# A filter unit's end given out between the next unit's first pieces, its norm summed in two parts, and one more place for weight preparation

## The chip, the core and the metric

The kernel runs on one core of a Trainium2 chip. The engines that matter here are TensorE (PE, with its weight loads shown apart as PEld), VectorE (DVE), ScalarE (ACT), GpSimd (POOL) and SyncE (SP), which issues most DMA transfers. Each engine works through its own instructions in order and waits on semaphores for the others. The metric is the device time of one execution in microseconds, the median of several runs; lower is better.

## What is computed

The program is a backbone of two layers over 2048 tokens of width 1024 with 256 context tokens. The even layer mixes a pooling branch with attention of 6 query heads over 2 key heads; the odd layer has a long convolution by FFT (Hyena) and a Fourier branch. The change touches the part that makes the filters of the long convolution, and the preparation of the odd layer's weights. Both run in the gaps of the even layer's attention. The filters are:

```python
h = (hdn @ w3).reshape(L, HY_ORDER, 2, HY_WIDTH)        # L 2048, order 2, width 768
h = h * decay[:, None, None, :]
h = h / (jnp.sum(jnp.abs(h), axis=(0, 2), keepdims=True) + EPS)
k = jnp.concatenate([h[:, :, 0], zero, h[:0:-1, :, 1]], axis=0)
...
zf = jnp.fft.rfft(z, n=2 * L, axis=1)
kf = jnp.fft.rfft(k, n=2 * L, axis=0)
return jnp.fft.irfft(zf * kf[None], n=2 * L, axis=1)[:, :L]
```

The norm of a channel, the sum of absolute values over all positions, is needed only at the end of a filter, where it also scales the skip term; the spectrum kf is what is stored for the odd layer.

## The kernel before, in words

The attention runs in 96 blocks (6 heads x 8 groups of rows x 2 halves). Each block is a string of tokens, written by hand in BLOCK: one string for even and one for odd blocks, and two shorter ones for the time when the side work is over. A token is a piece of a block: T transposes probabilities (PE), copies them out as ph (ACT) and takes the rest as pl (DVE); S multiplies scores (PE); M takes the row's highest value (DVE); E takes exponentials (ACT); Z sums them; V multiplies by values; D and N finish a block of rows: D makes the diagonal bdg (ACT) and prb (PE), N makes rb (DVE) and gives y<-rb to SP. At the end of a block SP gets the query loads qh, ql and bsg for a later block. Transposes have six PSUM buffers.

Between these pieces stand three tokens for side work. F (and f, in one pair of blocks out of eight) runs the filter generator up to its next yield, which is called a fill here; p runs one step of the weight preparation. Each engine gets its instructions in the order in which the tokens are reached, so the strings set the order of everything. after(n, fn) leaves a piece of work until n tokens later, or until the next fill at the latest.

The filter generator makes 12 units (6 groups of 128 channels x 2 orders). A unit has 8 groups of positions. For each, PE makes hacc (L1194), DVE multiplies by the decay into ht (L1195, two buffers) and reduces absolute values into one of eight slots of rd (L1198); in a second fill PE makes the first DFT stage fa from ht (L1231) and ACT copies it into fX three tokens later (L1232). At the last group, DVE sums the eight slots into rs (L1204), PE spreads that sum (smacc, L1207 and L1208), DVE makes the scale sc_n and puts the skip term into ht (L1213 to L1218), makes sum and difference sd (L1219, L1220), PE makes fa from sd (L1229), and the last copy fills fX. A unit takes 18 fills. The matmul results hacc, smacc, fa and fnp of all side work share one PSUM buffer.

When fX is complete the rest of its FFT is put on a list of 48 POOL operations, which some() gives out at each fill for an estimated FFT_US of 4.4 us, and FFT_LATE, 4 calls of some() later, SP gets the store spec<-fX (2 MB, L1143). fX has two buffers (FILTER_X), the FFT's intermediate fT one. The skip row skr (512 B) is fetched with the filter weights, two units deep.

The weight preparation multiplies a piece by its gate on POOL, rounds it to wodd on ACT (L1409), takes the rest on POOL and stores wodd (wo, wi); its last part makes fnp on PE from the DFT matrix and the Fourier branch's weights (L1446) and copies it to fnM. When the filter generator is done, fill() runs whatever is left of the preparation at once and then opens the pools for the output projection, whose pieces fill the last blocks.

Of the kernel before, what the change touches and what calls it, by code (L numbers as in the profile page):

```python
# [20 lines left out]
P = 128  # L21
D = 1024
# [4 lines left out]
EPS = 1e-6  # L27
# [9 lines left out]
NCH = HW_ // P  # L37
N2 = 16
# [3 lines left out]
PAIRS = [(n, N2 - n) for n in range(1, 8)] + [(0, 8)]  # L42

BLOCK = [
# [204 lines left out]
def tile_net(ctx, tc, i, k, out, keep=None):  # L249
    nc = tc.nc  # L250
    v, s, g, pe, sy = nc.vector, nc.scalar, nc.gpsimd, nc.tensor, nc.sync
# [36 lines left out]
    specd = [[dram(f"spec{j}_{o}", (P, 2, N2, P)) for o in range(2)] for j in range(NCH)]  # L288
# [211 lines left out]
    with ExitStack() as st, tc.manual_schedule(engines=EVERY):  # L500
        sp = pool(st, "a_sb", 2)
# [617 lines left out]
    def filters(st, psum, tag, after):  # L1119

        fc = pool(st, "f_c2", 1, side="right")
        sp = pool(st, "f_u", 1, side="right")
        dft = fc.tile([P, N2, 2, P], F32, name="fdft")
        late, ops = [], []
        got, room = {}, [0.0]

        def some():

            due[0] += 1
            room[0] = min(room[0] + FFT_US, FFT_US)
            while ops and room[0] > 0:
                us, op = ops.pop(0)
                room[0] -= us
                if callable(op):
                    op()
                else:  # L1140
                    late.append((due[0] + FFT_LATE, op))
            if late and late[0][0] <= due[0]:
                sy.dma_start(*late.pop(0)[1])  # L1143

        due = [0]

        def fetch(u, grp):
            dec = sp.tile([P, 2, P], F32, tag="dec", name="dec", bufs=2)
            sy.dma_start(dec, k["decay"][u // 2, grp])
            hd = sp.tile([P, 2, P], F32R, tag="hd", name="hd", bufs=2)  # L1150
            n, m = PAIRS[grp]
            mv(hd, hdd[:, n : m + 1 : m - n, :])
            got[u, grp] = dec, hd

        def fetch_w3(u):
# [6 lines left out]
            skr = sp.tile([1, P], F32, tag="skr", name="skr", bufs=2)  # L1162
            sy.dma_start(skr, i["hy_skip"][0, o : o + 1, jl])
            got[u] = raw, skr

        def split_w3(u):
            raw, skr = got[u]
# [3 lines left out]
            got[u] = w, skr  # L1171
# [7 lines left out]
        for u in range(2 * NCH):  # L1179
            j, o = u // 2, u % 2  # L1180
            w3, skr = got.pop(u)
            rd = sp.tile([P, 8, P], F32, tag="rd", name="rd")
            X = sp.tile([P, 2, N2, P], F32, tag="X", name="fX", bufs=FILTER_X)
            for grp, (n, m) in enumerate(PAIRS):
                last = grp == 7
                if (u, grp) != (2 * NCH - 1, 7):
                    fetch(u + grp // 7, (grp + 1) % 8)
                dec, hd = got.pop((u, grp))
                ht = sp.tile([P, 2, 2, P], F32, tag="ht", name="ht", bufs=2)
                acc = psum.tile([P, 2, 2, P], F32, tag=tag, name="hacc")  # L1190
                for q in range(2):
                    for x in range(2):
                        w = w3[:, x, ::-1] if q else w3[:, x]
                        pe.matmul(acc[:, q], hd[:, q, :], w, start=x == 0, stop=x == 1)  # L1194
                after(1, lambda: v.tensor_mul(ht, acc, dec.unsqueeze(2).to_broadcast([P, 2, 2, P])))  # L1195
                yield
                some()
                v.tensor_reduce(out=rd[:, grp, :], in_=ht.rearrange("p a d b -> p b (a d)"), axis=AX.X, op=ALU.add,  # L1198
                                apply_absolute_value=True)
                if u + 1 < 2 * NCH and grp in (3, 6):  # L1200
                    (fetch_w3 if grp == 3 else split_w3)(u + 1)
                if last:
                    rs = sp.tile([P, P], F32, tag="rs", name="rs")
                    v.tensor_reduce(out=rs, in_=rd.rearrange("p a b -> p b a"), axis=AX.X, op=ALU.add)  # L1204
                    yield
                    sm = psum.tile([P, 512], F32, tag=tag, name="smacc")
                    pe.matmul(sm[:, 0:1], rs, ones[:, 0:1], start=True, stop=True)  # L1207
                    pe.matmul(sm[0:1, P : 2 * P], ones[:, 0:1], rs, start=True, stop=True)  # L1208
                    sd = sp.tile([P, 2, 2, P], F32, tag="ht", name="sd", bufs=2)

                    def scaled():
                        idx = o * NCH + j
                        v.tensor_scalar(out=sc_n[:, idx : idx + 1], in0=sm[:, 0:1], scalar1=EPS, scalar2=None, op0=ALU.add)  # L1213
                        rw = sp.tile([1, P], F32, tag="rw", name="rw")
                        v.scalar_tensor_tensor(out=rw, in0=sm[0:1, P : 2 * P], scalar=EPS, in1=skr, op0=ALU.add, op1=ALU.mult)
                        v.reciprocal(sc_n[:, idx : idx + 1], sc_n[:, idx : idx + 1])
                        v.tensor_add(ht[0:1, 0, 0, :], ht[0:1, 0, 0, :], rw)
                        v.memset(ht[0:1, 0, 1, :], 0.0)  # L1218
                        v.tensor_add(sd[:, 0], ht[:, :, 0], ht[:, :, 1])  # L1219
                        v.tensor_sub(sd[:, 1], ht[:, :, 0], ht[:, :, 1])  # L1220


                    after(2, scaled)
                    yield
                fa = psum.tile([P, 2, 2, P], F32, tag=tag, name="fa")
                for r in range(2):
                    for q, b in enumerate((n, m)):
                        if last:
                            pe.matmul(fa[:, r, q], dft[:, b, r, :], sd[:, r, q], start=True, stop=True)  # L1229
                        else:  # L1230
                            pe.matmul(fa[:, r], dft[:, b, r, :], ht[:, q], start=q == 0, stop=q == 1)  # L1231
                after(3, lambda: s.copy(X[:, :, n : m + 1 : m - n, :], fa))  # L1232
                yield
                if last:
                    T = sp.tile([P, 2, N2, P], F32, tag="T", name="fT")
                    ops += [(0.04 + 2.05 * us, fn) for fn, us in fft16(g, X, T, False, g, True)]
                    ops.append((0.0, (specd[j][o], X)))
                some()
        while ops or late:
            some()  # L1240
            yield
# [17 lines left out]
    with ExitStack() as st:  # L1259
# [195 lines left out]
        def after(n, fn):  # L1455

            pending.append([n, fn])
# [145 lines left out]
    with ExitStack() as st, tc.manual_schedule(engines=EVERY):  # L1603
# [222 lines left out]
    with ExitStack() as st, tc.manual_schedule(engines=EVERY):  # L1826
# [265 lines left out]
        with ExitStack() as fs:  # L2092
# [75 lines left out]
            for lb in range(2):  # L2168
# [251 lines left out]
```

## Time and profile before

| | before |
|---|---|
| median of 3 runs (lowest, highest) | 3173.49 us (3167.7, 3178.07) |
| profiled execution: time, span | 3180.38 us, 3178.6 us |
| PE busy | 2935.4 us (92%), 16969 instructions |
| PEld busy | 2519.8 us (79%) |
| DVE busy | 2146.7 us (68%) |
| ACT busy | 1325.2 us (42%) |
| POOL busy | 1131.8 us (36%) |
| mean granted clock of TensorE | 0.968 |

The profiled execution is one run with the profiler on; its own time is the 3180.38 us, 6.9 us above the median of the runs without a profile. PE has the largest share, but a share over the whole span says little of one stage. The attention with the filters between its pieces lies between about 620 and 1620 us of the span, the end of the filters, the output projection and the rest of the even layer behind it. What is to be read is the idle time of PE in that stretch, and what released it: in a row of the timeline the brackets name that idle time, the engine that ended it, and the tile and line that it wrote.

### The profile page before, as it was taken

How to read it: one execution, taken by the hardware profiler on the slowest of the kernel's cores; microseconds unless marked ns; L12 is line 12 of the kernel's file. 1: busy time of each engine (PE TensorE's matmuls, PEld its weight loads, DVE VectorE, ACT ScalarE, POOL GpSimd, SP SyncE). 2: the span in 40 equal slices, each digit the busy share in tenths (PEclk: the TensorE clock that was granted, in tenths of full speed). 3: DMA queues.
4: the chain of work that ended last, by engine and by line, in shares of the span. 5: the costliest groups of instructions: out<-in, count | busy, mean ns of one | idle time of the engine just before them, and what ended most of it. 6: DMA issues, size and time to landing. Idle time of an engine off the chain costs nothing. (4 is left out here: it accounts for less than half of the span.)

```text
span 3178.6 us, 46875 instructions
## 1 busy us (share of the span) xinstructions
PE 2935.4 (92%) x16969; PEld 2519.8 (79%) x16969; DVE 2146.7 (68%) x3981; ACT 1325.2 (42%) x3047; POOL 1131.8 (36%) x1091
## 2 busy tenths in 40 slices
PE   7899999799999999999986999999989999988799
PEld 4898888688888888888875778777878787874577
DVE  4676436477777777777764343377789797978556
ACT  4444545365555555555554232322323222232223
POOL 3122222127768787777772344001010000101110
PEclk9999999899999999999998999999999999999899
DMA  6466335533433334333325676688898989876875
GB/s 219 149 203 206 119 134 165 177 98 123 128 124 120 110 121 131 112 107 113 114 77 193 213 265 244 241 267 275 267 310 272 292 280 307 274 251 184 217 206 175
DMA packets 346707, 602.74 MB, mean 190 GB/s; under 512 B 41894, under 2 KB 216168, under 8 KB 336490
## 3 DMA queue, kind: packets, MB, share of 16 engines
q1 hardware_dynamic: 321322, 516.63, 47.8%
q0 software_dynamic: 25152, 83.10, 11.2%
q8 instruction: 134, 2.20, 0.3%
q14 instruction: 99, 0.81, 0.1%
HBM read 376.80 MB, written 187.18 MB: 177 GB/s over the span
## 5 line engine op out<-in xcount | busy, mean ns | idle before, releaser
L312 DVE TENSOR_TENSOR pl<-pt,ph 128x512 fp32r<-128x512 f32 (+1 forms) x480 | 300.1, 634 | 160.0 <-ACT ph L309 153.6
L155 DVE TENSOR_TENSOR gB<-gB 128x256 f32<-128x256 f32 (+3 forms) x442 | 351.6, 845 | 51.5 <-ACT gB L1927 47.7
L1334 ACT ACTIVATE pb<-S,mx 128x512 f32<-128x512 f32 (+1 forms) x480 | 310.7, 658 | 177.5 <-DVE mx L1326 143.3
L315 PE MATMUL dacc<-dh,dw 128*128 128x512 f32 x768 | 311.4, 405 | 46.5 <-DMA dh<-h1T 45.4
L309 ACT CAST ph<-pt 128x512 fp32r<-128x512 f32 (+1 forms) x480 | 256.2, 557 | 216.9 <-PE pt L1345 215.0
L316 PE MATMUL dacc<-dh,dw 128*128 128x512 f32 x768 | 304.4, 396 | 0.0
L317 PE MATMUL dacc<-dh,dw 128*128 128x512 f32 x768 | 304.1, 396 | 0.0
L1323 DVE TENSOR_REDUCE mx<-S 128x1 f32<-128x512 f32 (+1 forms) x480 | 279.5, 629 | 8.9 <-PE S L317 8.7
L1345 PE MATMUL pt<-ident,pb 128*128 128x128 f32 x1728 | 251.3, 275 | 21.4 <-ACT pb L1334 20.0
L312 POOL TENSOR_TENSOR wl<-raw,wh 128x256 fp32r<-128x256 f32 x160 | 134.8, 873 | 373.3 <-ACT wh L309 347.6
L1357 PE MATMUL o<-ph,vh 128*128 128x256 f32 x864 | 237.9, 306 | 0.2
L1345 PEld LDWEIGHTS pt<-ident,pb 128*128 128x128 f32 x1728 | 200.2, 141 | 41.3 <-ACT pb L1334 29.8
L315 PE MATMUL S<-kh,qh 128*128 128x512 f32 (+1 forms) x480 | 200.0, 417 | 30.1 <-DVE pl L312 15.4
L1358 PE MATMUL o<-ph,vl 128*128 128x256 f32 x864 | 220.4, 286 | 1.8 <-DMA vl<-vl 1.8
L155 POOL TENSOR_TENSOR fX<-fT 128x256 f32<-128x256 f32 (+2 forms) x168 | 219.2, 1328 | 2.6
L315 PEld LDWEIGHTS dacc<-dh,dw 128*128 128x128 f32 x768 | 147.7, 192 | 85.0 <-DMA dh<-h1T 43.4
L155 POOL TENSOR_TENSOR fT<-fX 128x1024 f32<-128x1024 f32 (+2 forms) x120 | 190.8, 1622 | 58.4 <-ACT fX L1232 56.6
L315 PE MATMUL acc<-wh,hh 128*128 128x256 f32 x672 | 198.8, 296 | 5.4 <-DVE hh L311 2.6
L317 PE MATMUL acc<-wh,hl 128*128 128x256 f32 x672 | 194.0, 289 | 1.0 <-DVE hl L312 0.9
L316 PE MATMUL acc<-wl,hh 128*128 128x256 f32 x672 | 194.1, 289 | 0.9 <-POOL wl L312 0.8
L316 PE MATMUL S<-kl,qh 128*128 128x512 f32 (+1 forms) x480 | 182.2, 379 | 1.3 <-DMA kl<-kT1l 1.3
L317 PE MATMUL S<-kh,ql 128*128 128x512 f32 (+1 forms) x480 | 181.9, 379 | 0.0
(475 smaller groups left out, 7397.5 us busy)
## 6 DMA issues: line engine op xcount, KB each, us to landing
dh<-h1T SPq DMA_DIRECT2D x172, 512.0 KB
spec<-fX SPq DMA_DIRECT2D x12, 2048.0 KB
dw<-wi SPq DMA_DIRECT2D x48, 512.0 KB
gK<-spec SPq DMA_DIRECT2D x48, 512.0 KB
raw<-in_ev_w_in_dram SPq DMA_DIRECT2D x160, 128.0 KB
u<-dev SPq DMA_DIRECT2D x70, 256.0 KB
cu<-u POOLq DMA_DIRECT2D x17, 1024.0 KB, 8.3
wmb<-in_w_mod_dram SPq DMA_DIRECT2D x16, 1024.0 KB
```

Of the source, the lines that this page charges most:

```text
L155: put(out, lambda: v.tensor_tensor(out=out, in0=in0, in1=in1, op=op))
L309: s.copy(hi, src)
L312: lo_eng.tensor_sub(lo, src, hi.bitcast(F32))
L315: pe.matmul(acc, ah, bh, start=first, stop=False)
L316: pe.matmul(acc, ah, bl, start=False, stop=False)
L317: pe.matmul(acc, al, bh, start=False, stop=last)
L1323: v.tensor_reduce(out=B["mx"][:, c : c + 1], in_=S[:, :n], axis=AX.X, op=ALU.max)
L1334: s.activation(B["pb"][:, c * 512 : c * 512 + n], B["S"][c][:, :n], AF.Exp, bias=B["mx"][:, 5:6], accum_out=B["sm"][:, c : c + 1])
L1345: pe.transpose(pt[:, t, :], B["pb"][:, (4 * c + t) * P : (4 * c + t + 1) * P], ident)
L1357: pe.matmul(gr["o"], vh[:, a, :], ph[:, t, :], start=a == 0, stop=False)
L1358: pe.matmul(gr["o"], vl[:, a, :], ph[:, t, :], start=False, stop=False)
```

## The change

The last group's tail is cut out of its unit. norm (smacc, scale, skip term, sd), the last group's spectrum and the start of the FFT of unit u are now given out between the first pieces of unit u + 1: behind its features(0), behind its spectrum(0), and before its features(1). Only the last unit has its tail by itself. The sum over slots is taken in two parts: at group 4 over slots 0 to 4 into slot 5, at group 7 over the four slots 2 to 5 (later groups reuse slots from 2 on) into slot 0; rd has six slots, and rs is gone. ht has three buffers. The skip row is fetched at group 6, into one buffer. A unit takes 17 fills in place of 18. Even blocks get one more p at their end, so a pair of blocks has seven in place of six.

```diff
 BLOCK = [
-    "T0 p S0 S1 F S2 S3 S4 M T1 f p F D V3 V4 E1 N E3 T2 E0 T3 p E4 E2 F T4 Z",
+    "T0 p S0 S1 F S2 S3 S4 M T1 f p F D V3 V4 E1 N E3 T2 E0 T3 p E4 E2 F T4 p Z",
...
-            rd = sp.tile([P, 8, P], F32, tag="rd", name="rd")
-            X = sp.tile([P, 2, N2, P], F32, tag="X", name="fX", bufs=FILTER_X)
...
-                ht = sp.tile([P, 2, 2, P], F32, tag="ht", name="ht", bufs=2)
...
-                if last:
-                    rs = sp.tile([P, P], F32, tag="rs", name="rs")
-                    v.tensor_reduce(out=rs, in_=rd.rearrange("p a b -> p b a"), axis=AX.X, op=ALU.add)
-                    yield
-                    sm = psum.tile([P, 512], F32, tag=tag, name="smacc")
...
-                    after(2, scaled)
-                    yield
-                fa = psum.tile([P, 2, 2, P], F32, tag=tag, name="fa")
...
+            ht = st_[grp] = sp.tile([P, 2, 2, P], F32, tag="ht", name="ht", bufs=3)
...
+        def sums(st_, grp):
+
+            u, rd = st_["u"], st_["rd"]
+            v.tensor_reduce(out=rd[:, grp - 3 * (grp > 4), :], in_=st_[grp].rearrange("p a d b -> p b (a d)"), axis=AX.X, op=ALU.add,
+                            apply_absolute_value=True)
...
+            if grp == 6:
+                st_["skr"] = fetch_skip(u)
+            if grp in (4, 7):
+                lo, hi, to = (0, 5, 5) if grp == 4 else (2, 6, 0)
+                v.tensor_reduce(out=rd[:, to, :], in_=rd[:, lo:hi].rearrange("p a b -> p b a"), axis=AX.X, op=ALU.add)
...
+            after(2, scaled)
+            after(3, both)
...
+            after(3, lambda: s.copy(X[:, :, n : m + 1 : m - n, :], fa))
...
+        last = None
+        for u in range(2 * NCH + 1):
+            st_ = None
+            if u < 2 * NCH:
+                w3 = got.pop(u)
+                st_ = {"u": u, "w3": w3, "rd": sp.tile([P, 6, P], F32, tag="rd", name="rd")}
+                features(st_, 0)
+            yield
+            some()
+            if last:
+                norm(last)
+                yield
+            if st_:
+                sums(st_, 0)
+                spectrum(st_, 0)
+            if last or st_:
+                yield
+                some()
+            if last:
+                spectrum(last, 7)
...
+                transform(last)
...
+            for grp in range(1, 8):
+                features(st_, grp)
+                yield
+                some()
+                sums(st_, grp)
+                if grp < 7:
+                    spectrum(st_, grp)
+                    yield
+                    some()
+            last = st_
```

On DVE at the end of a unit in the middle of the filters, before (rd and rs are the unit's last sums, L1213 and L1215 its scale; pl, mx, sm and r belong to the attention):

```order
L1198 TENSOR_REDUCE rd<-ht 128x128
L1204 TENSOR_REDUCE rs<-rd 128x128
L312 TENSOR_TENSOR pl<-pt,ph 128x2x128
L1329 TENSOR_REDUCE sm<-sm 128x1
L1330 RECIPROCAL r<-sm 128x1
L312 TENSOR_TENSOR pl<-pt,ph 128x4x128
L1323 TENSOR_REDUCE mx<-S 128x1 x2
L312 TENSOR_TENSOR pl<-pt,ph 128x4x128
L1323 TENSOR_REDUCE mx<-S 128x1 x3
L1326 TENSOR_REDUCE mx<-mx 128x1
L1213 TENSOR_SCALAR sc_n<-smacc 128x1
L1215 SCALAR_TENSOR_TENSOR rw<-smacc,skr 1x128
```

And at such an end now:

```order
L1200 TENSOR_REDUCE rd<-ht 128x128
L1208 TENSOR_REDUCE rd<-rd 128x128
L1195 TENSOR_TENSOR ht<-hacc,dec 128x512
L312 TENSOR_TENSOR pl<-pt,ph 128x4x128
L312 TENSOR_TENSOR pl<-pt,ph 128x2x128
L1380 TENSOR_REDUCE sm<-sm 128x1
L1381 RECIPROCAL r<-sm 128x1
L312 TENSOR_TENSOR pl<-pt,ph 128x4x128
L1374 TENSOR_REDUCE mx<-S 128x1 x3
L1220 TENSOR_SCALAR sc_n<-smacc 128x1
L1222 SCALAR_TENSOR_TENSOR rw<-smacc,skr 1x128
L1223 RECIPROCAL sc_n<-sc_n 128x1
```

The next unit's first ht stands between the sum and the scale now; sd follows in both.

On ACT at the end of the weight preparation, before (wodd is a prepared weight, fnM the Fourier branch's, the rest is attention):

```order
L1334 ACTIVATE pb,sm<-S,mx 128x512
L1334 ACTIVATE pb,sm<-S,mx 128x256
L309 CAST ph<-pt 128x4x128 x2
L1409 CAST wodd<-wraw 128x512 x2
L1448 COPY fnM<-fnp 128x512 x2
L1366 ACTIVATE bdg<-ident,r 128x128 x2
L1334 ACTIVATE pb,sm<-S,mx 128x512 x2
```

Now the last of them stands by itself, one in each of two blocks:

```order
L1385 ACTIVATE pb,sm<-S,mx 128x512
L1385 ACTIVATE pb,sm<-S,mx 128x256
L309 CAST ph<-pt 128x4x128
L1499 COPY fnM<-fnp 128x512
L309 CAST ph<-pt 128x4x128
L1417 ACTIVATE bdg<-ident,r 128x128 x2
L1385 ACTIVATE pb,sm<-S,mx 128x512 x2
```

Four pieces of the preparation that stood in a row at one place of one block are spread over the blocks ahead.

On ACT, the first copy of unit 4 into fX now, with what each waits for (DMAHW is a DMA queue, where the store of unit 2 from the same buffer is meant):

```order
L309 CAST ph<-pt 128x4x128 [waits PE_49,Activation_49]
L1417 ACTIVATE bdg<-ident,r 128x128 x2
L1246 COPY fX<-fa 128x2x2x128 [waits DMAHW6_49,PE_49,Pool_49]
L1385 ACTIVATE pb,sm<-S,mx 128x512 [waits DVE_49]
L1385 ACTIVATE pb,sm<-S,mx 128x512
```

On SP, the rows up to that store:

```order
L261 DMA wi_6_183<-wodd 128x1024 [waits DMAHW7_49,Pool_49]
L1477 DMA wgb<-gate_227 128x512 [waits DMAHW0_49]
L1480 DMA wraw<-in_ev_w_out_dram 128x512 [waits DMAHW1_49]
L261 DMA y_85<-rb 128x256 [waits DMAHW2_49,DVE_49]
L261 DMA qh<-qT1h 128x256 [waits DMAHW3_49,PE_49]
L261 DMA ql<-qT1l 128x256 [waits DMAHW4_49,PE_49]
L1351 DMA bsg<-sg_3_78 128x256 [waits DMAHW5_49]
L1143 DMA spec_0_151<-fX 128x4096 [waits DMAHW6_49]
```

Before, the same store stood thus, and the first copy of the unit that reuses its buffer came in a later block:

```order
L261 DMA qh<-qT1h 128x256 [waits DMAHW1_49,PE_49]
L261 DMA ql<-qT1l 128x256 [waits DMAHW2_49,PE_49]
L1300 DMA bsg<-sg_3_78 128x256 [waits DMAHW3_49]
L261 DMA wi_4_181<-wodd 128x1024 [waits DMAHW4_49,Pool_49]
L497 DMA wraw<-in_od_w_in_dram 128x2x128 [waits DMAHW5_49]
L497 DMA wraw<-in_od_w_in_dram 128x2x128 [waits DMAHW6_49]
L1143 DMA spec_0_151<-fX 128x4096 [waits DMAHW7_49]
```

The copy of the new unit is reached, in the order of tokens, between the last blocks' work and the store's place behind y, qh, ql and bsg; before, it came after the store.

More of the change, by code (lines that the diff above doesn't have):

```diff
@@ L1170, in split_w3, with fetch_skip @@
             v.tensor_sub(w[:, 1], raw, w[:, 0].bitcast(F32))
-            got[u] = w, skr
+            got[u] = w
+        def fetch_skip(u):
+            skr = sp.tile([1, P], F32, tag="skr", name="skr")
+            sy.dma_start(skr, i["hy_skip"][0, u % 2 : u % 2 + 1, u // 2 * P : u // 2 * P + P])
+            return skr
         fetch(0, 0)
@@ L1178, in filters, with features @@
         yield
-        for u in range(2 * NCH):
-            j, o = u // 2, u % 2
-            w3, skr = got.pop(u)
-            rd = sp.tile([P, 8, P], F32, tag="rd", name="rd")
-            X = sp.tile([P, 2, N2, P], F32, tag="X", name="fX", bufs=FILTER_X)
[L1184 to L1188, printed above, removed]
-                ht = sp.tile([P, 2, 2, P], F32, tag="ht", name="ht", bufs=2)
[L1190 to L1195, printed above, removed]
+        def features(st_, grp):
+            u = st_["u"]
+            if (u, grp) != (2 * NCH - 1, 7):
+                fetch(u + grp // 7, (grp + 1) % 8)
+            dec, hd = got.pop((u, grp))
+            w3 = st_["w3"]
+            ht = st_[grp] = sp.tile([P, 2, 2, P], F32, tag="ht", name="ht", bufs=3)
+            acc = psum.tile([P, 2, 2, P], F32, tag=tag, name="hacc")
+            for q in range(2):
+                for x in range(2):
+                    w = w3[:, x, ::-1] if q else w3[:, x]
+                    pe.matmul(acc[:, q], hd[:, q, :], w, start=x == 0, stop=x == 1)
+            after(1, lambda: v.tensor_mul(ht, acc, dec.unsqueeze(2).to_broadcast([P, 2, 2, P])))
@@ new lines, in sums @@
+        def sums(st_, grp):
+            u, rd = st_["u"], st_["rd"]
+            v.tensor_reduce(out=rd[:, grp - 3 * (grp > 4), :], in_=st_[grp].rearrange("p a d b -> p b (a d)"), axis=AX.X, op=ALU.add,
+                            apply_absolute_value=True)
+            if u + 1 < 2 * NCH and grp in (3, 6):
+                (fetch_w3 if grp == 3 else split_w3)(u + 1)
+            if grp == 6:
[3 more added lines that the diff above has]
+                v.tensor_reduce(out=rd[:, to, :], in_=rd[:, lo:hi].rearrange("p a b -> p b a"), axis=AX.X, op=ALU.add)
@@ new lines, in norm, with scaled, both @@
+        def norm(st_):
+            u, ht, rs = st_["u"], st_[7], st_["rd"][:, 0, :]
+            idx = u % 2 * NCH + u // 2
+            sm = psum.tile([P, 512], F32, tag=tag, name="smacc")
+            pe.matmul(sm[:, 0:1], rs, ones[:, 0:1], start=True, stop=True)
+            pe.matmul(sm[0:1, P : 2 * P], ones[:, 0:1], rs, start=True, stop=True)
+            sd = st_["sd"] = sp.tile([P, 2, 2, P], F32, tag="ht", name="sd", bufs=3)
+            def scaled():
+                v.tensor_scalar(out=sc_n[:, idx : idx + 1], in0=sm[:, 0:1], scalar1=EPS, scalar2=None, op0=ALU.add)
+                rw = sp.tile([1, P], F32, tag="rw", name="rw")
+                v.scalar_tensor_tensor(out=rw, in0=sm[0:1, P : 2 * P], scalar=EPS, in1=st_["skr"], op0=ALU.add, op1=ALU.mult)
+                v.reciprocal(sc_n[:, idx : idx + 1], sc_n[:, idx : idx + 1])
+                v.tensor_add(ht[0:1, 0, 0, :], ht[0:1, 0, 0, :], rw)
+                v.memset(ht[0:1, 0, 1, :], 0.0)
+            def both():
+                v.tensor_add(sd[:, 0], ht[:, :, 0], ht[:, :, 1])
+                v.tensor_sub(sd[:, 1], ht[:, :, 0], ht[:, :, 1])
+            after(2, scaled)
+            after(3, both)
@@ new lines, in spectrum @@
+        def spectrum(st_, grp):
+            if "X" not in st_:
+                st_["X"] = sp.tile([P, 2, N2, P], F32, tag="X", name="fX", bufs=FILTER_X)
+            X, (n, m) = st_["X"], PAIRS[grp]
+            fa = psum.tile([P, 2, 2, P], F32, tag=tag, name="fa")
+            for r in range(2):
+                for q, b in enumerate((n, m)):
+                    if grp == 7:
+                        pe.matmul(fa[:, r, q], dft[:, b, r, :], st_["sd"][:, r, q], start=True, stop=True)
+                    else:
+                        pe.matmul(fa[:, r], dft[:, b, r, :], st_[grp][:, q], start=q == 0, stop=q == 1)
+            after(3, lambda: s.copy(X[:, :, n : m + 1 : m - n, :], fa))
@@ new lines, in transform @@
+        def transform(st_):
+            u, X = st_["u"], st_["X"]
+            T = sp.tile([P, 2, N2, P], F32, tag="T", name="fT")
+            ops.extend([(0.04 + 2.05 * us, fn) for fn, us in fft16(g, X, T, False, g, True)])
+            ops.append((0.0, (specd[u // 2][u % 2], X)))
+        last = None
[14 more added lines that the diff above has]
+            if last or st_:
@@ L1196, in filters @@
                 yield
                 some()
[L1198 to L1201, printed above, removed]
-                if last:
-                    rs = sp.tile([P, P], F32, tag="rs", name="rs")
-                    v.tensor_reduce(out=rs, in_=rd.rearrange("p a b -> p b a"), axis=AX.X, op=ALU.add)
-                    yield
-                    sm = psum.tile([P, 512], F32, tag=tag, name="smacc")
[L1207 to L1220, printed above, removed]
-                    after(2, scaled)
-                    yield
@@ L1225, in filters @@
-                fa = psum.tile([P, 2, 2, P], F32, tag=tag, name="fa")
[L1226 to L1232, printed above, removed]
@@ L1233, in filters @@
-                yield
[L1234 to L1238, printed above, removed]
+            if last:
[3 more added lines that the diff above has]
+                some()
+            if st_ is None:
+                break
+            for grp in range(1, 8):
[5 more added lines that the diff above has]
+                    spectrum(st_, grp)
+                    yield
+                    some()
```

6 lines of the change are left out of this document (2 added, 4 removed).

## The prediction

> **What bounds the kernel now.** I read the page's slices first, then the attention stage, which the change touches, in windows.
>
> ```profile
> span 3178.6 us, 46875 instructions
> PE   7899999799999999999986999999989999988799
> 950.00:1000.00 50.00, 49.77 (x335) 45.65 (x334) 37.86 (x75) 29.48 (x78) 49.16 (x40) 1.00 0.30 93
> 1000.00:1050.00 50.00, 47.16 (x316) 41.61 (x315) 39.44 (x77) 27.69 (x73) 34.99 (x23) 1.00 0.41 137
> 1650.00:1700.00 50.00, 34.80 (x213) 29.95 (x211) 24.89 (x53) 21.32 (x57) 35.81 (x34) 0.89 0.36 124
> 1700.00:1750.00 50.00, 35.90 (x215) 31.05 (x216) 20.73 (x44) 21.18 (x55) 1.37 (x2) 0.81 0.59 220
> ```
>
> A windows row gives the stretch, its length, then busy time of PE, weight loads, DVE, ACT and POOL, the granted clock, and the DMA share and GB/s. PE bounds this stage: it is busy 49.8 of 50 us where no filter unit ends, 47.2 where one does, and loses about 15 us in each of the two stretches behind the last unit. So only PE's idle time can be won, and a new wait that reaches PE is paid in full.
>
> **Gain 1: the weight preparation is no longer rushed.** Before, steps of it are left when the filters end, and all are issued at once between two pieces of one block. With seven places in two blocks instead of six it ends beforehand; the last groups then stand among other work (the rows on ACT above).
>
> ```profile
> 1641.37 0.50 PE L315 MATMUL S<-kh,qh 128*128 128x512 f32 x1 [2.13 <-DVE pl L312]
> 1663.62 0.62 ACT L1409 CAST wodd<-wraw 128x512 fp32r<-128x512 f32 x1 [4.88 <-POOL wraw L1431]
> 1665.50 0.79 PE L315 MATMUL S<-kh,qh 128*128 128x512 f32 x1 [4.57 <-DVE pl L312]
> 1665.50:1671.40 5.90, 5.90 (x18) 5.03 (x19) 4.34 (x10) 1.22 (x6) 5.75 (x9) 0.50 0.00 0
> 1689.71 0.60 PE L1345 MATMUL pt<-ident,pb 128*128 128x128 f32 x4
> 1707.12 3.75 PE L1446 MATMUL fnp<-wraw 128*128 128x256 f32 x8 [16.81 <-DMA wraw<-cst_dftd_dram]
> 1714.82 3.75 PE L1446 MATMUL fnp<-wraw,wft 128*128 128x256 f32 x8 [3.95 <-DMA wft<-cst_dftd_dram]
> 1718.01 0.78 PE L1357 MATMUL o<-ph,vh 128*128 128x256 f32 x1
> ```
>
> A timeline row is start, duration, engine, line, instruction, and in brackets the idle time ahead and its releaser. From 1690.31 (1689.71 + 0.60) to 1718.01, 27.7 us, PE does two groups of fnp and else nothing. They cost 3.75 us each here; in the 0.50 row the granted clock is half of the 1.00 above, and at 1.00 they would need about 1.9 each, 3.8 together, which they still cost where they stand now. 27.7 - 3.8, and an estimated 1 us for the cold start behind it, is **25**. Ahead of the rush the last unit's FFT fills POOL; weight pieces queue behind it, ACT waits 4.88 us for one, and PE stands 2.13 and 4.57 us. Behind the second it runs 5.9 us at half clock, 2.9 lost. In the new order preparation is over before that FFT. 2.13 + 4.57 + 2.9: **9.6**.
>
> **Gain 2: the unit ends.** PE's waits by releaser, 690 to 1620 us (us in total, times, longest), and two rows of DVE's reductions (least/mean/most ns, first and last start):
>
> ```profile
> PE fa L1229 <- DVE sd L1219: 7.8, 4, 2.8
> PE smacc L1207 <- DVE rs L1204: 6.3, 6, 1.9
> PE S L315 <- DVE pl L312: 5.2, 4, 1.3
> PE S L315 <- DVE sm L1329: 2.6, 2, 1.3
> L1204 DVE TENSOR_REDUCE rs<-rd x12: 1884/1922/2007, 689.9 to 1608.1; 128x128 f32<-128x1024 f32 x12
> L1198 DVE TENSOR_REDUCE rd<-ht x96: 1029/1070/1106, 627.1 to 1607.0; 128x128 f32<-128x512 f32 x96
> ```
>
> These four make 21.9 us. A unit's end was one train on DVE (rd 1.07, rs 1.92, sd) and PE between its parts. Now 1.2 us of the sum (five of eight slots of 1.92) runs at group 4, and at the end a reduction over four slots, of rd's shape, 1.07, stands between other pieces; norm, scaling and sd come two fills apart. I take three quarters, **16**; between 0 (the new unit's hacc and rd wait there in their stead) and 21.9. The third ht buffer, six slots for eight and the skip row's own fetch at group 6 cost no engine time on PE; that fetch is wanted four or more fills later, and a fill comes every 4.64 us:
>
> ```profile
> L1213 DVE TENSOR_SCALAR sc_n<-smacc x12: 148/148/151, 695.4 to 1614.6; 128x1 f32<-128x1 f32 x12
> ```
>
> (1614.6 - 695.4) / (11 units x 18 fills) = 4.64. If it were late, DVE would stand and PE behind it; with 18 us of lead I take 0. The seventh p itself adds no work, only brings it forward: its casts stand nearer to their POOL multiplications, up to 2 us of ACT waits in all; I take **-2**.
>
> **The loss: two buffers of fX, and a unit now restarts sooner.** A unit's first copy into fX needs the buffer of the unit two back, so it waits until that unit's store to spec has landed. Unit 0:
>
> ```profile
> 697.88 0.59 ACT L1232 COPY fX<-fa 128x512 f32<-128x512 f32 x1 [1.59 <-PE fa L1229]
> 698.54 4.73 POOL L155 TENSOR_TENSOR fT<-fX 128x1024 f32<-128x1024 f32 x2 [7.87 <-ACT fX L1232]
> 759.93 2.53 POOL L155 TENSOR_TENSOR fX<-fT 128x512 f32<-128x512 f32 x2
> 773.72 0.57 SPq L1143 DMA_DIRECT2D spec<-fX  x1
> 790.02 0.59 ACT L1232 COPY fX<-fa 128x512 f32<-128x512 f32 x1 [0.50 <-PE fa L1231]
> 1371.84 0.42 SPq L1143 DMA_DIRECT2D spec<-fX  x1
> 1381.89 0.60 ACT L1232 COPY fX<-fa 128x512 f32<-128x512 f32 x1
> GB/s 215 174 236 311 615 451 498 382 492 382 437 437 382 492 273 601 273 601 273 601 55 55 0 0 0 0 0 0 0 0 0 0 0 0 0 0 0 0 0 0
> ```
>
> Last copy of unit 0 at 697.88, FFT on POOL until 762.46, store at 773.72, first copy of unit 2 at 790.02: 20 fills, 92.1 us behind the last copy. In the new order group 7's copy comes after group 0 of the next unit, and 16 fills lie between: 16 x 4.64 = 74.3 us, so 772.2, about when SP issues the store, and the FFT is no shorter. The store's landing is not in the trace. The copy at 1381.89 does not wait 10.05 us behind its store: the upper bound. The last row is the GB/s in slices of 0.3 us from 1606.8, just where the store of 1606.85 starts: traffic stops 6.6 us later, a lower bound. I take 7. There are ten such copies (units 2 to 11), in three kinds by what stands around them (the rows on SP above: spec is queued behind y<-rb, q and weight stores):
>
> ```profile
> 1599.60 0.51 SPq L261 DMA_DIRECT2D wo<-wodd  x1
> 1600.17 0.60 SPq L1429 DMA_DIRECT2D wraw<-in_od_w_out_dram  x1
> 1601.58 0.69 ACT L1366 ACTIVATE bdg<-ident,r 128x128 f32<-128x128 f32 x2
> 1603.47 0.61 PE L1374 MATMUL prb<-bdg,ones 128*128 128x128 f32 x4
> 1604.57 0.42 DVE L1377 TENSOR_TENSOR rb<-o,rb 128x256 f32<-128x256 f32 x1
> 1606.38 0.69 DVE L312 TENSOR_TENSOR pl<-pt,ph 128x512 fp32r<-128x512 f32 x1 [0.47 <-ACT ph L309]
> 1606.85 0.42 SPq L1143 DMA_DIRECT2D spec<-fX  x1
> 1607.35 0.89 ACT L309 CAST ph<-pt 128x256 fp32r<-128x256 f32 x2
> 1610.40 0.50 PE L315 MATMUL S<-kh,qh 128*128 128x512 f32 x1 [1.29 <-DVE sm L1329]
> 1173.09 0.61 PE L315 MATMUL S<-kh,qh 128*128 128x512 f32 x1 [2.26 <-DMA kh<-kT1h]
> 1175.01 0.80 PE L316 MATMUL S<-kl,qh 128*128 128x512 f32 x1 [1.31 <-DMA kl<-kT1l]
> ```
>
> An even block of before, with a store in it, serves as measure. Kind 1 (units 4 and 7): the copy stands right behind bdg, ahead of the block's exps, and the store behind that same block's y<-rb. ACT is free at 1602.3, rb ends at 1605.0, the store goes at 1606.85 and lands at 1613.9; copy 0.59 and one exp 0.69 later, at 1615.2, PE has work again; it had some until prb's end at 1604.1. 11 us each; unit 7's takes in the load wait of 2.26 + 1.31 that stands there now. 22 - 3.6, and 2.5 us each for half clock behind it (2.9 in Gain 1; a part of it falls where PE would wait anyway): **23**. Kind 2 (units 5, 8, 11): the copy at the even block's end, ACT free at 1608.2, landing 1613.9, then copy 0.59, cast 0.45, pl 0.69: the next S at 1615.5 in place of 1610.4. 5 us, with a weight store and loads ahead on SP in two of three (0.51 + 0.60 each, up to 1.7) 6 to 7: 18, and 3 x 2.5 at half clock: **25.5**. Kind 3 (2, 3, 6, 9, 10): the store already lies ahead of that y; from 0 (landed beforehand) to 3 us (kind 2's 5.1 less the 1.9 that SP stands behind rb, 1604.99 to 1606.85), middle 1.7: **8.5**. Together 57, with the casts' 2, **59**: between 35 (landing just behind the traffic, kind 3 nil, no clock loss) and 80 (landing after 10).
>
> The half clock is a place where the Trainium skill speaks against this change. "TensorE: Matmul & The Clock Gate", Part 1, says that an idle window of some 3.4 us halves the clock, and that it takes about as long of steady work to come back. The trace agrees: 4.57 us idle, then 0.50. By the rule's own time the loss behind a wait would be 1.7 us in place of 2.5, and the sum some 4 us lower; the same page would leave today's waits under 3 us unpunished.
>
> "DMA: Bandwidth & Descriptors", in its fit of a transfer's time, puts about 2 us of fixed cost on a DMA, mostly the receipt of the write before its semaphore rises. No run here shows the landing; if the receipt came behind the 6.6 us of traffic, each store would land 1.5 us later, an estimate, and the sum would be some 8 us higher.
>
> **Sum.** Gains 25 + 9.6 + 16 = 50.6 (36 to 59); losses 59 (35 to 80): +8. The profiled execution took 3180.38, so 3188 beside it; it lies 6.9 above the median of the three runs, 3173.49, and by that the time is **3182**.
>
> **Rivals.** *The copies hide* (0.28): PE has six psT buffers of transposes and scores ahead of ACT, and SP may issue the store early; kind 2 and kind 3 then reach nothing and only kind 1 costs 23. For it: kind 2's 5 us are near what is queued. Against: ACT runs in order, and casts behind the copy feed the next S. 3173.5 - 51 + 23 = 3146 (3123 to 3160). *Every copy pays* (0.17), the one that ends on the slower side for sure: kind 3 also waits the whole landing, because hacc and fa share one psF buffer and the next hacc waits until the copy has emptied it. It decides once the store goes less than 7 us ahead of the copy, as when a weight store that waits for POOL stands ahead of spec. Five more times 7.2 - 1.7 is 27: 3209. Against: four of the five copies have a block's half between y and them. *The unit ends still wait* (0.10): hacc of the next unit and norm share psF, so PE meets the same DVE train; gain 2 is nil: 3198.
>
> **How the numbers follow.** My forecast has 0.45, with 3160 to 3203 of its own (landing at 8.5 or 5.5, gain 2 from 5 to 20). 0.3% is 9.5 us, about what a measurement of this kernel can tell from no change: below 3164 is faster, above 3183 slower. The forecast gives 0.05, 0.20 and 0.20 to faster, same, slower; the first rival 0.28 faster; the second 0.17 slower; the third 0.02 same, 0.08 slower. Faster 0.33, same 0.22, slower 0.45. The range runs from 3135 to 3212: it leaves out a third of the first rival, some 0.09, a third of the second, 0.06, and a rest.
>
> **What would show it.** Right: in the new trace the first copies of units 4 and 7 wait 9 to 11 us and those of 5, 8 and 11 about 5, each released by the DMA spec<-fX; PE idles there and shows 0.5 clock after; no idle stretch between the last unit and the next stage is above 5 us; fnp stands at about 1.9 us a group; smacc and sd no longer release PE. Wrong: copies released by PE, as now (my landing or the order on SP is off); PE busy through the copies' waits (they hide); or an idle PE behind sc_n. A landing above 9 us would take the time over 3195, one below 5 under 3165.

## The result, and the profile after

The changed kernel took 3206.21 us (median of 4 runs, 3200.23 to 3206.86), the kernel before 3175.78 us in the same comparison: 30.4 us slower by these medians (a ratio of 1.0096). The ratio on record is a little higher, 1.0112, with a 95% interval of 1.0088 to 1.0135, which is 28 to 43 us. The forecast was 3182 with a range of 3135 to 3212: slower was its likelier side, but by 8 us, and the time lies 24 us above the forecast and 6 us below the upper end of the range.

The page's slices and the windows that were shown of before, now of the changed kernel (stretch, length, busy PE, weight loads, DVE, ACT, POOL, clock, DMA share, GB/s):

```profile
span 3204.1 us, 46849 instructions
PE   7999999798989897899899999999999999988799
950.00:1000.00 50.00, 43.64 (x277) 40.04 (x278) 31.31 (x59) 26.51 (x69) 35.57 (x26) 0.88 0.30 94
1000.00:1050.00 50.00, 36.59 (x228) 32.79 (x227) 29.73 (x60) 21.40 (x56) 29.45 (x29) 0.87 0.34 116
1650.00:1700.00 50.00, 47.59 (x319) 41.90 (x318) 33.45 (x70) 29.41 (x79) 48.99 (x44) 1.00 0.23 69
1700.00:1750.00 50.00, 44.55 (x311) 39.52 (x310) 33.79 (x71) 32.11 (x83) 3.40 (x3) 1.00 0.68 253
```

The two stretches behind the filters are full now: 47.6 and 44.6 us in place of 34.8 and 35.9. The filter stage has holes that it did not have, 43.6 and 36.6 us of PE in place of 49.8 and 47.2, and a clock below 0.9 in both. PE's waits between the first and the last unit's end (us in total, times, longest):

```profile
PE S L315 <- DVE pl L312: 34.2, 8, 12.1
PE pt L1396 <- ACT pb L1385: 29.0, 20, 12.4
PE smacc L1215 <- DVE ht L1195: 8.9, 5, 3.6
PE fa L1243 <- ACT fX L1246: 5.9, 3, 3.1
```

None of these rows names a DMA. Behind the first two stands a chain that one has to follow back: PE waits for pl or pb, these wait on ACT, and ACT waits in front of a copy into fX. The view of the tile spec says who waited for the stores of the spectrum:

```profile
who waited for it (us, times):
  ACT fX L1246: 75.3, 9
```

In the kernel before no copy into fX did (the other rows of that view, in both kernels, are of the odd layer, which loads spec). One of these waits, the first copy of unit 4, in the timeline of PE, SP and ACT:

```profile
943.21 0.60 PE L1425 MATMUL prb<-bdg,ones 128*128 128x128 f32 x4
944.77 0.32 SPq L261 DMA_DIRECT2D y<-rb  x1
946.58 0.42 SPq L1143 DMA_DIRECT2D spec<-fX  x1
954.75 0.58 ACT L1246 COPY fX<-fa 128x512 f32<-128x512 f32 x1 [14.91 <-DMA spec<-fX]
956.07 1.11 PE L1396 MATMUL pt<-ident,pb 128*128 128x128 f32 x4 [11.08 <-ACT pb L1385]
```

SP gives out the store 1.8 us behind y; it has landed 8.2 us later, when the copy starts; ACT has waited 14.9 us, and PE 11.1 for the exponential behind the copy. The copy of unit 5 stands at the end of a block, and there a cast and pl pass the wait on to the scores:

```profile
1037.62 0.95 SPq L1143 DMA_DIRECT2D spec<-fX  x1
1047.10 0.58 ACT L1246 COPY fX<-fa 128x512 f32<-128x512 f32 x1 [9.86 <-DMA spec<-fX]
1048.95 0.58 PE L315 MATMUL S<-kh,qh 128*128 128x256 f32 x1 [8.89 <-DVE pl L312]
```

The other large ones are units 7, 8 and 11:

```profile
1222.22 0.58 ACT L1246 COPY fX<-fa 128x512 f32<-128x512 f32 x1 [16.36 <-DMA spec<-fX]
1223.54 1.12 PE L1396 MATMUL pt<-ident,pb 128*128 128x128 f32 x4 [12.45 <-ACT pb L1385]
1317.74 0.58 ACT L1246 COPY fX<-fa 128x512 f32<-128x512 f32 x1 [12.54 <-DMA spec<-fX]
1319.59 0.58 PE L315 MATMUL S<-kh,qh 128*128 128x256 f32 x1 [12.10 <-DVE pl L312]
1563.46 0.58 ACT L1246 COPY fX<-fa 128x512 f32<-128x512 f32 x1 [7.10 <-DMA spec<-fX]
1565.31 0.58 PE L315 MATMUL S<-kh,qh 128*128 128x256 f32 x1 [6.13 <-DVE pl L312]
```

To see where time is lost and won, one instruction of each block serves as a milestone: the last reduction of the row's maximum on DVE (mx<-mx), 96 of them. Its start in each kernel against the kernel before, at the first, the 85th (at the end of the last unit before: its scale sc_n starts at 1614.6 too) and the last block:

| kernel (profiled execution) | 1st block | 85th | 96th | 1st to 85th | 85th to 96th |
|---|---|---|---|---|---|
| before, us | 616.6 | 1614.5 | 1762.5 | | |
| changed | -0.9 | +65.0 | +25.5 | +65.9 | -39.5 |

The change loses 65.9 us in the filter stage and wins 39.5 behind it; 26.4 is left. The experiments are measured by the same milestones. Each column rests on one profiled execution, and the base here is the one of 3180.38 us, while the kernel before took 3166 to 3171 us by its medians beside the experiments. So a milestone difference to the kernel before is good to some 10 us only (e3: 31.2 us by the spans, 17.1 by the medians); differences by medians are the surer ones.

### The profile page after: what moved, and what is told of

It is laid out like the page before. It is cut to its first block, busy times and chain, and to the rows that moved or that the text cites. A ratio compares the mean times of both kernels' runs of the same rounds, so it can differ in the third digit from the quotient of the medians.

```text
span 3204.1 us, 46849 instructions
## 1 busy us (share of the span) xinstructions
PE 2938.7 (92%) x16969; PEld 2525.1 (79%) x16969; DVE 2153.2 (67%) x3993; ACT 1324.4 (41%) x3047; POOL 1130.7 (35%) x1091
## 3 DMA queue, kind: packets, MB, share of 16 engines
q0 software_dynamic: 25152, 83.10, 11.1%
## 5 line engine op out<-in xcount | busy, mean ns | idle before, releaser
L155 DVE TENSOR_TENSOR gB<-gB 128x256 f32<-128x256 f32 (+3 forms) x442 | 351.6, 845 | 48.7 <-ACT gB L1978 44.8
```

The lines of the kernel that those rows point to most:

```text
L155: put(out, lambda: v.tensor_tensor(out=out, in0=in0, in1=in1, op=op))
```

## The experiments

All times are medians; the difference is to the kernel before as it ran on the same chip in the same comparison (3175.78 us for the changed kernel; 3168.95 for e1 to e4, 3166.43 for e5 to e8, 3170.75 for e9 and e10). The intervals are about 6 us to either side.

| run | median us | to before | ratio (95%) | 1st to 85th | 85th to 96th |
|---|---|---|---|---|---|
| changed | 3206.21 | +30.4 | 1.0112 (1.0088 to 1.0135) | +65.9 | -39.5 |
| e1 changed, store 1 call behind | 3139.84 | -29.1 | 0.9909 (0.9888 to 0.993) | +4.6 | -42.2 |
| e5 changed, store 2 calls behind | 3127.78 | -38.7 | 0.9881 (0.9865 to 0.9897) | -7.0 | -42.7 |
| e9 changed, store 3 calls behind | 3166.92 | -3.8 | 0.9995 (0.9977 to 1.0013) | +31.3 | -41.2 |
| e2 before, store 8 calls behind | 3256.97 | +88.0 | 1.0284 (1.0256 to 1.0311) | +88.7 | -11.3 |
| e3 before, seventh p | 3151.83 | -17.1 | 0.9951 (0.9931 to 0.997) | +12.8 | -36.1 |
| e4 before, sum in two parts | 3152.66 | -16.3 | 0.995 (0.9931 to 0.997) | -19.3 | -0.5 |
| e6 before, both | 3139.87 | -26.6 | 0.9922 (0.991 to 0.9934) | +2.6 | -37.7 |
| e7 as e6, store 1 call behind | 3141.42 | -25.0 | 0.9923 (0.991 to 0.9935) | +4.4 | -40.5 |
| e8 changed, no seventh p | 3233.85 | +67.4 | 1.0213 (1.0199 to 1.0227) | +44.4 | +10.7 |
| e10 as e5, no seventh p | 3176.88 | +6.1 | 1.0018 (1.0 to 1.0036) | -19.0 | +19.0 |

**e1: the store sooner.** If the landing of the store is the loss, giving it to SP sooner takes the loss away and leaves the rest of the change as it is.

```diff
-                    late.append((due[0] + FFT_LATE, op))
+                    late.append((due[0] + 1, op))
```

> The changed kernel with the store of a spectrum given to SP one call of some() behind the FFT's last piece instead of four, so about 14 us sooner (3 fills of 4.64). Theory A, the change loses by the landing of that store: the first copies of units 4, 5, 7, 8 and 11 wait under 4 us each for spec<-fX (9.9 to 16.4 and 7.1 now), the 65 us by which the changed kernel was behind at the 84th block go to between -15 and +5, its lead from the end of the filters stays, and the time is 3120 to 3145. Theory B, the moved pieces themselves cost PE (smacc behind ht, exponentials behind the scale on DVE): these waits stay as they are and the time stays above 3165. Theory C, the early store holds SP up until POOL is done, and decay and feature loads come late: waits for dec or hd of some us each, 3145 to 3165.

3139.84, in the range of theory A. No copy waits for spec any more, and the stage's loss falls from 65.9 to 4.6 us. Smacc still waits 8.9 us for ht, as in theory B, but that is small. A part of theory C is there too, at a load that it did not name: PE has one new wait of 4.87 us, and its chain begins at the store, which now stands on SP ahead of the FFT's end (rows of POOL, SP, ACT, DVE and PE):

```profile
1329.85 1.29 POOL L155 TENSOR_TENSOR fX<-fT 128x512 f32<-128x512 f32 x1
1331.17 0.33 SPq L1143 DMA_DIRECT2D spec<-fX  x1
...
1336.59 0.64 SPq L1480 DMA_DIRECT2D wraw<-in_od_w_out_dram  x1
...
1341.76 1.26 POOL L1482 TENSOR_TENSOR wraw<-wraw,wgb 128x512 f32<-128x512 f32 x1 [10.62 <-DMA wraw<-in_od_w_out_dram]
1343.06 0.62 ACT L1460 CAST wodd<-wraw 128x512 fp32r<-128x512 f32 x1 [6.33 <-POOL wraw L1482]
1344.19 1.02 DVE L312 TENSOR_TENSOR pl<-pt,ph 128x512 fp32r<-128x512 f32 x2 [6.46 <-ACT ph L309]
1344.94 0.78 PE L315 MATMUL S<-kh,qh 128*128 128x512 f32 x1 [4.87 <-DVE pl L312]
```

SP stands at the store until POOL's last piece ends at 1331.14; the load of wraw behind it goes late, POOL waits 10.6 us for it, ACT for POOL, PE for ACT.

**e2: the store later, in the kernel before.** The other direction, without any of the moved pieces.

```diff
-                    late.append((due[0] + FFT_LATE, op))
+                    late.append((due[0] + 8, op))
```

> The kernel before with the store eight calls of some() behind the FFT's last piece instead of four, nothing else: the store comes as close to the first copy of the unit two on as in the changed kernel, but none of the change's moved pieces is in it. Theory A: first copies wait for spec<-fX, 40 to 80 us in all, and the time is 3215 to 3255. Theory B: the store's place costs nothing by itself, under 3185.

3256.97, 2 us beyond theory A's range. All ten first copies wait for the store, two of them:

```profile
982.50 0.58 ACT L1232 COPY fX<-fa 128x512 f32<-128x512 f32 x1 [14.98 <-DMA spec<-fX]
1069.39 0.58 ACT L1232 COPY fX<-fa 128x512 f32<-128x512 f32 x1 [3.56 <-DMA spec<-fX]
```

So the wait alone, with nothing else of the change, makes the kernel slower by 88 us. Theory B, by which the store's place costs nothing by itself, falls.

**e3: the seventh p alone.**

```diff
-    "T0 p S0 S1 F S2 S3 S4 M T1 f p F D V3 V4 E1 N E3 T2 E0 T3 p E4 E2 F T4 Z",
+    "T0 p S0 S1 F S2 S3 S4 M T1 f p F D V3 V4 E1 N E3 T2 E0 T3 p E4 E2 F T4 p Z",
```

> The kernel before with the seventh place for weight preparation alone. If the rush behind the filters (27.7 us without PE but for two groups of fnp) and the two stalls ahead of it are what that place removes: 25 to 35 us faster, 3140 to 3150, with no idle PE stretch above 5 us behind the last unit. If the preparation's work just costs the same elsewhere: within 10 us of 3175.

3151.83: between the two. Behind the filters it wins 36.1 us, as foreseen, but ahead of them it loses 12.8 (by the medians, 17.1 won in all, it would be nearer 19). Some of that can be read off PE's waits, above all a longer one for the second half's keys (2.26 + 1.31 us before) and new ones for a feature load:

```profile
PE S L315 <- DMA kh<-kT1h: 7.3, 1, 7.3
PE hacc L1194 <- DMA hd<-hdd: 3.6, 2, 2.4
```

The keys and hd are given out by SP, whose list now has the preparation's loads and stores more densely ahead of them. That SP's list is what makes them late was not tried by itself.

**e4: the sum in two parts alone.** In the kernel before, with the rest of a unit's end where it was.

```diff
-            rd = sp.tile([P, 8, P], F32, tag="rd", name="rd")
+            rd = sp.tile([P, 6, P], F32, tag="rd", name="rd")
...
+                if grp in (4, 7):
+                    lo, hi, to = (0, 5, 5) if grp == 4 else (2, 6, 0)
+                    v.tensor_reduce(out=rd[:, to, :], in_=rd[:, lo:hi].rearrange("p a b -> p b a"), axis=AX.X, op=ALU.add)
...
-                    rs = sp.tile([P, P], F32, tag="rs", name="rs")
-                    v.tensor_reduce(out=rs, in_=rd.rearrange("p a b -> p b a"), axis=AX.X, op=ALU.add)
+                    rs = rd[:, 0, :]
```

> The kernel before with the sum over slots in two parts alone (six slots, no rs). If the long reduction at a unit's end is what PE waits for there: the 6.3 us of smacc behind the sum and some of the 7.8 us of fa behind sd shrink, 4 to 10 us faster, 3166 to 3172. If the whole train counts and not that one reduction: within 4 us of 3175.

3152.66: more than expected. The waits for the sum and sd shrink as thought (smacc 6.3 to 3.2, fa 7.8 to 6.4), and the waits of the scores for pl, which stood behind the long reduction on DVE, go nearly altogether (5.2 to 0.4):

```profile
PE fa L1231 <- DVE sd L1221: 6.4, 4, 2.8
PE smacc L1209 <- DVE rd L1202: 3.2, 3, 1.1
PE S L315 <- DVE pl L312: 0.4, 1, 0.4
```

That is 9.3 us of the 19.3. The wait for the keys (3.6 us) is gone as well. The remaining 6 are not idle time: between the two milestones PE is busy 942.9 us where it was busy 949.7 before, and the granted clock was 0.50 for 6.8 us of this stretch, for 23.9 before.

**e5 and e9: the store two and three calls behind.** How the loss goes with the store's place.

```diff
-                    late.append((due[0] + FFT_LATE, op))
+                    late.append((due[0] + 2, op))
```

> The changed kernel with the store two calls of some() behind the FFT instead of four, 9.3 us sooner (one call sooner still it took 3139.8). Theory A, what counts is how long before the copy the store goes: waits of 12 to 16 us on ACT fall to 3 to 7, those of 10 or less go; units 4 and 7 still cost PE 2 to 4 us each, and the time is 3140 to 3155. Theory D, it is not the landing but the place of the store behind a y on SP, so that any sooner place gives all: 3136 to 3143.

3127.78: better than either theory said, and than e1. The copies of units 4 and 7 do not wait at all; two others still do, without a trace on the scores (PE waits 3.1 us in all at fa for a copy):

```profile
1333.66 0.58 ACT L1246 COPY fX<-fa 128x512 f32<-128x512 f32 x1 [3.49 <-DMA spec<-fX]
1410.96 0.58 ACT L1246 COPY fX<-fa 128x512 f32<-128x512 f32 x1 [5.08 <-DMA spec<-fX]
```

> The changed kernel with the store three calls of some() behind the FFT instead of four, 4.64 us sooner; two calls took 3127.8 and four 3206.2. Theory A, a copy's wait shrinks by as much as the store goes sooner: of the waits of PE, 3.4, 3.1, 11.1, 8.9, 2.5, 12.5, 12.1 and 6.1 us, 29 us go with some half clock behind them, so 3160 to 3178, with units 4 and 7 still at 6 to 8 us. Theory D, it is on or off by the store's place behind y on SP: near one of the two ends, under 3140 or over 3190.

3166.92, in the range of theory A, but not in its way. Seven copies still wait for spec, those of units 5, 8 and 11 by 9.92, 8.02 and 7.08 us, two of them as long as with four calls; those of units 4 and 7, which A left at 6 to 8 us, do not wait. The rows of SP show why. The store before unit 4's copy, then that before unit 5's:

```profile
929.07 0.46 SPq L1143 DMA_DIRECT2D spec<-fX  x1
939.21 0.32 SPq L261 DMA_DIRECT2D y<-rb  x1
...
1014.69 0.33 SPq L261 DMA_DIRECT2D y<-rb  x1
...
1017.77 0.77 SPq L1143 DMA_DIRECT2D spec<-fX  x1
```

The first has passed y and goes 10 us ahead of it, where it went 1.8 us behind; the second still stands behind y. So a store's time is set by what stands ahead of it in SP's list: y goes when DVE's rb is done, and a store behind it gains nothing by a fill less until it passes y. A and D each had half of it.

**e6 and e7: is the moved end worth anything?** The seventh p and the two-part sum together, in the kernel before; and the same with the early store (edits as above).

> The kernel before with the seventh place for weight preparation and the sum in two parts, without the unit's end moved into the next unit and with the store where it was. If the two add up (17.1 and 16.3 us by themselves): 3131 to 3141, which is no slower than the changed kernel with the early store, so the moved ends bring nothing. If the moved ends are worth the 10 us or more that the prediction gave the unit ends: over 3145 here against 3139.8 there.

> The run e6 with the store one call behind the FFT instead of four: all of the changed kernel with the early store except that a unit's end stands in its own unit. No copy waits for a store in e6, so sooner brings nothing: within 5 us of e6. What the changed kernel with the early store differs from it is the price of the moved ends alone: between 3139.8 minus 3131 and 3139.8 minus 3141. If the early store holds SP up: 5 to 15 us above e6.

3139.87 and 3141.42. The two parts do not quite add up (26.6 us for 17.1 and 16.3): the wait for the keys, which the two-part sum takes away by itself, is back with 7.4 us. The store's place brings nothing where no copy waits for it. Against e1 (3139.84) the moved ends bring nothing, against e5 (3127.78) 12 us. By milestones e5 is 14.6 us ahead of e6 from the first block to the last. Of the 11.6 us that e1 is behind e5 at the 85th block, 7.9 are PE's waits of the scores for pl (15.0 and 7.1 us), 4.9 of them the wait shown at e1. That the rest is also the price of a blocked SP is not shown: e7 has the store at the same place, and it is within 2 us of e6.

**e8 and e10: the change without the seventh p**, with the store four and two calls behind.

> The changed kernel without the seventh place for weight preparation. The filters end four blocks sooner than in the kernel before, two pairs with six steps each less, so that some 37 steps instead of 25 are left for the rush: 25 to 40 us come back behind the filters, and some 10 us less are lost ahead of them. 3220 to 3240. If the rush was no loss: 3190 to 3206.

> The changed kernel with the store two calls behind, without the seventh place for weight preparation. In the kernel before that place brought 17.1 us, 36 of them behind the filters and a loss of 11 ahead of them; with the filters over four blocks sooner the rush is longer (32.2 us of PE waiting for its loads in the run without the place, 16.8 before). If the place's cost and gain add to the rest: 35 to 45 us less the 8 to 11, 3152 to 3166. If the place costs nothing once the store is out of the way: 3160 to 3175.

3233.85, as expected, and 3176.88, 11 us beyond the first of the two ranges and 2 beyond the second. The rush is back, PE's wait in it is longer than the 16.8 us of before, and in e10 longer than in e8 (rows of e8, then of e10):

```profile
PE fnp L1497 <- DMA wraw<-cst_dftd_dram: 32.2, 1, 32.2
```

```profile
PE fnp L1497 <- DMA wraw<-cst_dftd_dram: 39.4, 1, 39.4
```

In these three pairs the seventh place is worth more, the longer that wait: by the differences to before 17 us in the kernel before, 37 with the store four calls behind (67.4 - 30.4) and 45 with it two behind (6.1 + 38.7).

## Why the prediction was right or wrong

**The bound** held. From the first to the 85th milestone, of before, of the changed kernel and of e5:

```profile
616.60:1614.50 997.90, 949.67 (x6351) 861.87 (x6352) 752.81 (x1463) 575.06 (x1495) 702.30 (x582) 0.98 0.38 121
615.70:1679.60 1063.90, 966.94 (x6369) 877.35 (x6370) 760.74 (x1483) 578.54 (x1503) 747.92 (x616) 0.95 0.37 118
612.10:1603.10 991.00, 947.39 (x6369) 859.69 (x6370) 760.87 (x1482) 577.60 (x1503) 747.60 (x616) 0.99 0.40 127
```

The change adds 48.7 us of idle PE (97.0 for 48.2) and 17.3 us of busy PE at a lower clock (0.95 for 0.98). Against e5, which has the same matmuls and differs by the store's place alone, it is 53.4 and 19.6.

**The main step held**: two buffers of fX, a restart four fills sooner, copies that wait for the landing of a store, in the three kinds that were named. e2 shows the wait alone to cost 88 us; e5 goes from the changed kernel's +65.9 at the 85th block to -7.0 by the store's place alone, 73 us (69 of the whole time by the medians).

**Its size was too small: 57 forecast, 73 measured.** Kind 1 was 11 us each, measured 11.08 and 12.45; that it came out so near is in part luck, since a later landing was made up for by a group of transposes that kept PE busy until 945.0, behind prb's end at 943.8. On ACT the waits of units 4 and 7 were 14.9 and 16.4 us, longer than the 9 to 11 given as the sign. Kind 2 was 18 us, measured 8.89 + 12.10 + 6.13 = 27.1, the kind that was off most: the landing was taken as 7 us, and in the nine waits it took 7.6 to 10.0, 8.7 in the mean (1047.10 - 1037.62 = 9.5 at unit 5). At unit 8 the store also went 3.5 us after ACT was free at 1305.20 (1317.74 - 12.54), behind two loads and a weight store that itself waited for POOL until 1306.56, as the second rival had it, though for another kind of copy:

```profile
1306.58 0.55 SPq L261 DMA_DIRECT2D we<-wodd  x1
1307.18 0.60 SPq L1477 DMA_DIRECT2D wgb<-gate  x1
1307.83 0.82 SPq L1480 DMA_DIRECT2D wraw<-in_od_w_out_dram  x1
1308.70 0.46 SPq L1143 DMA_DIRECT2D spec<-fX  x1
```

Kind 3 was 8.5, measured at PE 3.06 (unit 2) and 2.49 (unit 6), where fa waits for the copy; the three others hardly reached PE. Half clock was 2.5 us behind each of the five large waits, and nothing behind kind 3. The rows behind the waits of units 4 and 2:

```profile
956.00:961.00 5.00, 4.93 (x21) 4.73 (x22) 2.21 (x6) 4.80 (x14) 0.00 (x0) 0.50 0.00 0
788.30:794.30 6.00, 6.00 (x28) 6.00 (x29) 2.04 (x5) 4.22 (x12) 1.58 (x1) 0.50 0.01 2
```

Behind the five large waits PE worked 5.6, 4.9, 4.4, 3.9 and 3.9 us at 0.50 (units 4, 5, 7, 8, 11), which costs half of it, 1.9 to 2.8 and 2.3 in the mean; behind units 2 and 6 it worked 6.1 and 3.0, which is 4.6 us more that the forecast had put at nothing. The Trainium skill's "TensorE: Matmul & The Clock Gate", Part 1, has the clock back after at least one busy window of about 3.4 us, which would make it 1.7 at the least; all five took longer than that. The prediction also took from that page that waits under 3 us go unpunished, and the trace does not agree: in the kernel before PE stood 1.92 us for smacc at 1364.13, and the clock was 0.50 from 1364.4 to 1367.8. Waits of 23.5, 27.1 and 5.6 us and 16 at half clock are 72 of the 73. (The load wait of 3.6 us that the forecast let unit 7's copy take in is gone in e5 too, where that copy does not wait, so the store should not have been credited with it.)

The Trainium skill's other page that was weighed ("DMA: Bandwidth & Descriptors", the fit in "Anatomy of one DMA — SWDGE (gpsimd) path") gives an estimate of 6.8 us for 2 MB, for transfers that GpSimd issues, and the second reading, a receipt behind the traffic, gave 8.5. The 8.7 measured are near that, and so the sum 8 us higher was nearer, but not shown to be so for its reason. The traffic in slices of 0.3 us from 946.4, just ahead of the store of 946.58, goes on until 955.1, and the copy starts at 954.75:

```profile
GB/s 174 184 219 283 430 604 396 492 382 492 382 492 273 601 273 601 273 601 164 328 382 109 102 324 302 149 48 43 15 0 0 0 0 0 0 0 0 0 0 0
```

There 2.74 MB move and not the store alone; the loads dec and hd are given out right behind it. How much of the time to its landing is owed to that traffic was not tried.

**Gain 1 held**: 34.6 forecast, 39.5 measured from the 85th block on (36.1 in e3). The fnp groups stand alone and warm, the first:

```profile
1666.68 1.97 PE L1497 MATMUL fnp<-wraw 128*128 128x256 f32 x8
```

**The seventh p's price was mis-sized**: 2 us were given for casts on ACT, e3 shows 12.8 ahead of the 85th block. The place that I priced was the wrong one: not the casts, but loads that come late (7.3 us for the keys, 3.6 for hd) and others that were not taken apart.

**Gain 2 was too small**: 16 forecast; the two-part sum alone brings 16.3 in time, and the moved ends 12 more once the store is out of their way. But not by the way described: smacc is not free, it waits 8.9 us for ht, because hacc of the next unit's first group holds the one psF buffer until DVE has read it. The third rival had that, though not its size. (The gains' range of 36 to 59 does not follow from the terms either: 25 + 9.6 and 0 to 21.9 are 34.6 to 56.5.)

**The sum**, by the medians; a single run is good to some 6 us, so a difference of two or three to 8 or 10:

| term | forecast | measured | from |
|---|---|---|---|
| the store's landing | +57 | +69.1 | changed less e5 |
| the seventh p with the rush | -32.6 | -17.1 | e3 |
| the two-part sum and the moved ends | -16 | -28.4 | e4, and e5 less e6 |
| the first two parts do not add up | 0 | +6.8 | e6 less e3 and e4 |
| together | +8.4 | +30.4 | |

The store cost 12 us more than forecast, the seventh p won 15 less, and the ends won 12 more; that two parts got 7 in each other's way is no more than the error of that row. The direction rests on the store's landing, which was foreseen; that the time still fell into the range is in part luck, since the gain at the ends hid much of the other two errors, and a sum of +8 lies inside the 9.5 us that the prediction itself called no change. The row of e5 less e6 takes it that the store's place is worth nothing in e6, which e7 shows to within 2 us.

**The rivals**: the copies did not hide (9.86 us of wait on ACT at unit 5 came out as 8.89 on PE); the unit ends waited in part. The second rival's 3209 is the number nearest to the result, by luck: its way was that the five copies of kind 3 wait the whole landing, 27 us more on PE, and there they came to 5.6 (with the clock behind them some 10) where 8.5 were forecast; on ACT four of the five waited, 2.3 to 4.5 us.

**What beats both**: the changed kernel with the store two calls behind, 3127.78 us, ratio to before 0.9881 (0.9865 to 0.9897).

## What to carry to other kernels

Where a generator's units are made to follow each other more closely, look for the buffer that the unit after next needs (where there are two of it, as here), and for the whole way by which it comes free: the last transfer's place in its queue, what that queue waits for ahead of it, and the landing. A constant that was harmless (the store four calls behind) is then part of the change, and has to be set again; in this kernel four calls and three are too late, and the copies wait; at one call SP stood at the store, and a load behind it came late. The waits did not go in proportion to the calls: with one call less, unit 4's wait went altogether, as its store passed y in SP's list, and unit 5's stayed, as its store did not.

## What the runs showed of the hardware

A copy that waited for the landing of a 2 MB store from SBUF started 7.6 to 10.0 us after the store's issue began (nine copies of the changed kernel; 7.0 to 8.8 in the ten of e2), while in the row of the kernel before the traffic around such a store was over after 6.6 us. After a wait of 11.1 us the granted clock stayed at 0.50 for 5.6 us of work (956.07 to 961.64), after 8.9 us for 4.9, after 12.5, 12.1 and 6.1 us for 4.4, 3.9 and 3.9. Shorter waits of PE could do the same: 3.06 us (6.1 us at 0.50), 2.49 (3.0) and 1.92 (3.4, in the kernel before), but not all, since behind one of 1.85 us at 1214.23 before the clock was 1.00.
